# Block sums behind weight splits in the gate/up stages, and turned rows of q and y behind weight casts, in a hybrid decoder layer

## The chip, the cores and the metric

The kernel runs on one core of one Trainium2 chip. The metric is device time in microseconds (us) of one execution; the value given is the median of several. A core has five engines with a queue each: PE (TensorE, the matmuls), ACT (ScalarE), DVE (VectorE), POOL (GpSimd) and SP (SyncE, which only issues DMAs here).

## The reference

One decoder layer on 256 tokens, all in float32, model width 2048, FFN width 5632. Two half-step SwiGLU FFNs stand around a mixer of two attention branches.

```python
def _swiglu(x, w_gate, w_up, w_down):
    return (jax.nn.silu(x @ w_gate) * (x @ w_up)) @ w_down
...
    h = _layer_norm(ALPHA * h + 0.5 * _swiglu(h, ffn1_w_gate[l], ffn1_w_up[l], ffn1_w_down[l]), ln1_g[l], ln1_b[l])
    mix = _mixer(h, positions, w_in[l], ...)
    h = _layer_norm(ALPHA * h + mix, ln2_g[l], ln2_b[l])
    h = _layer_norm(ALPHA * h + 0.5 * _swiglu(h, ffn2_w_gate[l], ffn2_w_up[l], ffn2_w_down[l]), ln3_g[l], ln3_b[l])
```

The mixer projects h with w_in to queries and keys of low rank (rank 512, RMS-normed), to the queries, keys and values of a differential attention, and to two gates. Its first branch has 8 heads, each with a query of 128 plain columns and 64 rotated ones (RoPE). Its second branch has 4 heads of two score maps each, p0 - lambda * p1, with a distance bias (ALiBi). Each branch goes through an output product of its own, the two are multiplied by the sigmoid of their gates, summed to y, and y goes through w_out.

## The kernel before

**Splits.** The matmuls take operands of the type fp32r, and each float32 operand is given to them in two parts: `split` (L157) casts it on ACT to the high part (L158, CAST) and has DVE subtract that from the operand for the low part (L159, TENSOR_TENSOR). Each product is three matmuls (`triple`, L211): xh by wh (L212), xh by wl (L213), xl by wh (L214). So L213 is the first that needs the low part of a weight.

**The ring and the units.** Weights come from memory in tiles of 128 rows by 1024 columns, two blocks of 512. The split weights lie in a ring of pairs of tiles, `wring`: six pairs in the gate/up stages, ten elsewhere. A name such as `wring_16_118` is the high tile of a pair, `wring_17_119` its low tile; below, "slot 16" is the pair of the two. `next_pair` (L204) hands the pairs out in turn, so a cast into a pair has to wait until PE has done its last matmul on what the pair held. The work is cut into units. A unit has a load (a DMA on SP), a preparation (sums and split) and its matmuls; `unit` and `advance` (L177 to L203) pass it through these with a few units of lead between them, and `later(n, f)` (L107) puts a small step f behind the next n units.

**The gate/up pairs.** Each FFN has 11 pairs of a gate and an up tile of 512 columns. Pairs 1 to 10 go through the class `Hybrid` (L361). It multiplies the 2 by 2 blocks of a pair ("11", "12", "21", "22") by seven products in place of eight, as Strassen and Winograd do, and the rest of the pair by plain products. The seven products need sums of blocks, which `seventh` (L450) makes in its preparation: some by DMAs of GpSimd that accumulate (L468, L473), some on DVE (L466, in place on the loaded tile `sraw`). Six of the ten pairs (2, 3, 4, 6, 7, 8) are wide: each block has a third part, so a product with sums has three of them. The first sum belongs to the first part (s = 0), the second and the third are both issued in the preparation of the second part (s = 1). There are two such triples of sums in each wide pair.

**What sets the order.** A scheduler puts the instructions in the order of each engine's queue, by its own estimate of when they can run. `tc.issue_after(x)` adds one rule to that: what is issued inside it stands behind x if it is on the same engine. It adds no wait on another engine. `split_in_line` uses it to keep the splits on DVE in one line, and `behind_split(n)` (L354) puts an instruction behind the n-th last split. In before, each sum has `behind_split(s + 1)`. In the preparation of the second part this is the second-last split, the one ahead of the first part's. So the third sum may stand ahead of the first part's split.

**The mixer.** Rows are turned into columns by a DVE transpose of 32 by 32 blocks and a trip through memory on GpSimd's queue (`turn_out` L768, `turn` L779): a first DMA writes the blocks, a second reads them back into a tile `turned`, and a step some units later takes them. `turn_to_cols` (L792) takes them by an ACT copy (L795), for the rotated queries into `qrT` (`qr_done`, L1463) and for the keys into `kT`. `turn_to_quad` (L789) takes the rows of y by a split. The four differential heads come as steps scores, turn, values, turn2 (`diff_head`, L1402), spread over units by `later`; their exponentials are L1257 and L1258, the difference of the two maps L1420, and PE transposes the result at L1268.

Of the kernel before, what the change touches and what calls it, by code (L numbers as in the profile page):

```python
# [28 lines left out]
DH = 4  # L29
# [30 lines left out]
def layer_kernel(ctx: ExitStack, tc: tile.TileContext, a: dict, out: bass.AP):  # L60
# [6 lines left out]
    small = ctx.enter_context(tc.tile_pool(name="small", bufs=1))  # L67
# [4 lines left out]
    def nm(s):  # L72
        uid[0] += 1
        return f"{s}_{uid[0]}"

    def act_tile(shape, dt=F32, name="act"):
        return apool.tile(shape, dt, tag="act", name=nm(name), bufs=SLOTS)

    def tmp_tile(shape, name="tmp", dt=F32):
        return small.tile(shape, dt, tag="tmp", name=nm(name), bufs=6)  # L80
# [26 lines left out]
    def later(n, fn):  # L107
        uid[0] += 1
        heapq.heappush(todo, (step[0] + n, uid[0], fn))
# [45 lines left out]
    cast, lows, fetched, placed, weights = [None], [None], [None], [None], [None]  # L155
# [42 lines left out]
    def unit(load, prep, now, later_on=None):  # L198
        if load is not None:
            load()  # L200
        loaded.append((prep, now, later_on))
        advance(*ahead)

    def next_pair():  # L204
        assert len(ring) > len(prepared) + lag[0], (len(ring), len(prepared), lag[0])
        catch_up(len(ring) - 1)
        pair = ring.pop(0)
        ring.append(pair)
        return pair

    def triple(o, xh, xl, wh, wl, first, last, again=False):  # L211
        PE.matmul(o, xh, wh, start=first, stop=False, skip_group_check=again)  # L212
        PE.matmul(o, xh, wl, start=False, stop=False, skip_group_check=again)  # L213
        PE.matmul(o, xl, wh, start=False, stop=last, skip_group_check=again)  # L214
# [139 lines left out]
    def behind_split(n):  # L354
        return tc.issue_after(line[-n].ins) if len(line) >= n else nullcontext()

    def split_in_line(strict, *a):
        with behind_split(1) if strict else nullcontext():
            line.append(split(*a))

    class Hybrid:  # L361
# [42 lines left out]
        def group(self, w0, w1, done, wide=0, seeded=False, gates=False):  # L404
            banks = {}
            small = self.small
# [22 lines left out]
            def bank(n):  # L429
                first = n not in banks  # L430
                if first:
                    banks[n] = tr_bank() if n == "Z" and not small else mm_bank()
                return banks[n], first
# [9 lines left out]
            def source(name, s):  # L443
                w, j0 = blocks[name]
                return w[j0 + s] if s < 2 else w[4 + j0 // 2][:, :wide * 512]

            def stored(name, s):
                return R[name][s] if s < 2 else R[name][s][:, :wide * 512]

            def seventh(p, s):  # L450
                load_block, src, add, b = plan[p]
                st = {}
                tiles = G if s < 2 else wide

                def load():
                    if s < 2 and load_block in there:
                        return
                    nc.sync.dma_start(stored(load_block, s), source(load_block, s))

                def prep():  # L460
                    t = stored(src, s)
                    last = None
                    if add is not None:
                        for i in {0: (0,), 1: tuple(range(1, end_s + 1)), 2: ()}[s]:
                            with nullcontext() if small else behind_split(s + 1):
                                last = V.tensor_tensor(out=stored(src, i), in0=stored(src, i), in1=stored(add[1], i), op=ALU.add)  # L466
                    if p == 6 and p in added:
                        nc.gpsimd.dma_start(stored("22", s), source("12", s), accum_op=ALU.add)  # L468
                    pair = [v[:, :tiles * 512] for v in next_pair()]
                    with tc.issue_after(last.ins) if last is not None and not small else nullcontext():  # L470
                        split_in_line(not small, *pair, t)
                    if p == 1 and p in added:
                        nc.gpsimd.dma_start(stored("11", s), source("12", s), accum_op=ALU.add)  # L473
                    st["pair"] = [v.rearrange("p (g n) -> p g n", g=tiles) for v in pair]

                def now():
                    o, first = bank(b)
                    wh, wl = st["pair"]
                    for g in range(tiles):
                        if s < 2:  # L480
                            xh, xl = (v[:, 2 * s + g, :] for v in self.seven.at_[p])
                        else:
                            xh, xl = (v[:, g, :] for v in self.extra.at_[p])
                        triple(o, xh, xl, wh[:, g, :], wl[:, g, :], first and g == 0,
                               s == end_s and g == tiles - 1 and p in stops, b in "XZ" or seeded)
                    if s == end_s and p in after:
                        after[p]()
                unit(load if load_block else None, prep, now)
# [42 lines left out]
            turn = {n: iter(PLAIN[wide]) for n in range(2)}  # L531
# [236 lines left out]
    def turn_out(row, to):  # L768

        t = tmp_tile([P, 512], "blocks")  # L770
        V.transpose(t, row)  # L771
        for i in range(4):
            nc.gpsimd.dma_start(to.rearrange("(g r) (i f) -> i r g f", g=4, i=4)[i],  # L773
                                t[32 * i:32 * (i + 1), :].rearrange("r (g f) -> r g f", g=4))

    def turned(v):
        return v.rearrange("p (i k c) -> p k i c", i=4, k=4)

    def turn(row, use, wait, more):  # L779
        to = dram.tile([P, 512], F32, name=nm("turn"))  # L780
        turn_out(row, to)

        def back():
            t = tmp_tile([P, 512], "turned")
            nc.gpsimd.dma_start(t, to)
            later(more, lambda: use(turned(t)))
        later(wait, back)

    def turn_to_quad(row, b, x, q, wait, more):  # L789
        turn(row, lambda t: x.put(q, b, t), wait, more)  # L790

    def turn_to_cols(row, dst, b, wait, more, pinned=False):  # L792
        def use(t):
            with tc.issue_after(cast[0].ins) if pinned else nullcontext():
                S.copy(dst[:, :, b * P:(b + 1) * P].rearrange("p k (i c) -> p k i c", i=4), t)  # L795
        turn(row, use, wait, more)
# [432 lines left out]
    def rope(dst1, dst2, src, b, heads):  # L1229
        v = src.rearrange("p (h j i) -> p h j i", h=heads, j=2)  # L1230
        n = heads * ROPE
        tc_ = tmp_tile([P, heads, 2, HALF], "ropec")
        ts_ = tmp_tile([P, heads, 2, HALF], "ropes")
        sin = sincos[:, b, 0, :].unsqueeze(1).unsqueeze(1).to_broadcast([P, heads, 2, HALF])
        cos = sincos[:, b, 1, :].unsqueeze(1).unsqueeze(1).to_broadcast([P, heads, 2, HALF])
        V.tensor_tensor(out=tc_, in0=v, in1=cos, op=ALU.mult)
        V.tensor_tensor(out=ts_, in0=v, in1=sin, op=ALU.mult)
        V.tensor_tensor(out=dst1, in0=tc_[:, :, 0, :], in1=ts_[:, :, 1, :], op=ALU.subtract)
        V.tensor_tensor(out=dst2, in0=ts_[:, :, 0, :], in1=tc_[:, :, 1, :], op=ALU.add)
# [48 lines left out]
    def mixer(x, norm):  # L1288
# [47 lines left out]
        def cols_proj(w, xx, kt, name, k0=0, more=4, pinned=False):  # L1336
            dst = act_tile([P, 4, T], F32, name)

            def done(b, bank):
                t = tmp_tile([P, 512], name + "r")  # L1340
                S.copy(t, bank)
                later(1, lambda: turn_to_cols(t, dst, b, 4, more, pinned))
            project(w, xx, kt, 512, done, k0)
            return dst
# [111 lines left out]

        for h in range(DH):
            for i, f in enumerate(diff_head(h)):
                later(2 + 5 * h + 3 * i + i // 3, f)
        qT = [cols_proj(a["wuq"][c], cn, 4, "qT") for c in range(2)]  # L1460
        qrT = act_tile([P, 4, T], F32, "qrT")

        def qr_done(b, bank):  # L1463
            t = tmp_tile([P, 512], "qr")
            tv = t.rearrange("p (j h i) -> p j h i", j=2, h=MH)
            rope(tv[:, 0], tv[:, 1], bank, b, MH)
            later(1, lambda: turn_to_cols(t, qrT, b, 4, 4))
        project(a["wuq"][2], cn, 4, 512, qr_done)
        kT = [cols_proj(a["wuk"][c], cn, 4, "kT", 4, 6, True) for c in range(2)]
        v = [act_tile([P, 1024], F32, "v") for _ in range(2)]  # L1470
# [211 lines left out]
```

## Time and profile before

| what | us |
| --- | --- |
| median of 3 runs | 1958.54 (1957.15 to 1961.01) |
| the profiled execution | 1957.34 |
| its span | 1955.6 |
| PE busy in FFN1 up to 440 us | 438.45 of 440 |
| PE busy from 440 to 900 us | 459.69 of 460 |
| PE busy from 900 to 1340 us | 438.62 of 440 |
| PE busy from 1340 to 1700 us (FFN2's gate/up) | 359.77 of 360 |
| PE busy from 1700 us to the end | 246.45 of 255.6 |

A group row of the profile reads: line, engine, operation, written tile <- read tiles, shapes, count, then busy time and the mean of one in ns. A row of the timeline reads: start, duration, engine, line, operation, tiles, count of instructions that follow each other in the row; in brackets stands the engine's idle time before it, with what ended that. PE's matmuls overlap, so their pace is read from their starts.

### The profile page before, as it was taken

How to read it: one execution, taken by the hardware profiler on the slowest of the kernel's cores; microseconds unless marked ns; L12 is line 12 of the kernel's file. 1: busy time of each engine (PE TensorE's matmuls, PEld its weight loads, DVE VectorE, ACT ScalarE, POOL GpSimd, SP SyncE). 2: the span in 40 equal slices, each digit the busy share in tenths (PEclk: the TensorE clock that was granted, in tenths of full speed). 3: DMA queues.
4: the chain of work that ended last, by engine and by line, in shares of the span. 5: the costliest groups of instructions: out<-in, count | busy, mean ns of one | idle time of the engine just before them, and what ended most of it. 6: DMA issues, size and time to landing. Idle time of an engine off the chain costs nothing.

```text
span 1955.6 us, 25740 instructions
## 1 busy us (share of the span) xinstructions
PE 1943.0 (99%) x8715; PEld 1609.0 (82%) x8715; DVE 1760.4 (90%) x2117; ACT 1276.4 (65%) x1636; POOL 377.0 (19%) x610
## 2 busy tenths in 40 slices
PE   9999999999999999999999999999999999999998
PEld 8888888888888888888888888888888888888886
DVE  7999999999898879988987677789999999998987
ACT  6677676776655666666667655566767676666652
POOL 0122212321100010102241530012221122210110
PEclk9999999999999999999999999999999999999999
DMA  9988997988877667767676798688988888888973
GB/s 333 295 239 244 271 303 236 239 269 279 313 245 240 215 218 269 262 201 241 198 260 203 221 306 276 200 298 247 252 256 282 279 233 245 274 303 253 320 249 124
DMA packets 152244, 498.30 MB, mean 255 GB/s; under 512 B 22016, under 2 KB 22320, under 8 KB 152112
## 3 DMA queue, kind: packets, MB, share of 16 engines
q1 hardware_dynamic: 110592, 371.64, 52.9%
q0 software_dynamic: 41376, 124.89, 27.2%
q8 instruction: 68, 1.11, 0.2%
q14 instruction: 64, 0.52, 0.1%
q10 hardware_dynamic: 144, 0.13, 0.0%
HBM read 466.16 MB, written 30.41 MB: 254 GB/s over the span
## 4 chain that ended last, share of the span: by engine, by line
PE 94%; DVE 4%; DMA 1%; issue 1%; ACT 0%; SPq 0%; DVEq 0%
PE mm L213 26%; PE mm L214 26%; PE mm L212 26%; PE tr L213 4%; PE tr L214 4%; PE tr L212 4%; DVE wring L159 2%; DVE sraw L466 1%; PE tr L729 1%; DMA sraw<-in_gu_dram 0%; DMA xraw<-in_xT_dram 0%; PE tr L1483 0%; PE tr L1411 0%; PE tr L1485 0%; DMA raw<-in_gu_dram 0%
## 5 line engine op out<-in xcount | busy, mean ns | idle before, releaser
L158 ACT CAST wring<-sraw 128x1024 fp32r<-128x1024 f32 (+1 forms) x576 | 568.2, 1009 | 188.4 <-PE mm L214 69.8
L159 DVE TENSOR_TENSOR wring<-sraw,wring 128x1024 fp32r<-128x1024 f32 (+1 forms) x576 | 651.1, 1165 | 22.1 <-ACT wring L158 19.3
L158 ACT CAST wring<-raw 128x1024 fp32r<-128x1024 f32 (+2 forms) x436 | 448.7, 1035 | 281.2 <-PE mm L214 198.3
L159 DVE TENSOR_TENSOR wring<-raw,wring 128x1024 fp32r<-128x1024 f32 (+2 forms) x436 | 518.3, 1197 | 93.3 <-ACT wring L158 90.7
L212 PE MATMUL mm<-wring,h 128*128 128x512 f32 (+2 forms) x1152 | 443.5, 385 | 0.0
L213 PE MATMUL mm<-wring,h 128*128 128x512 f32 (+2 forms) x1152 | 442.7, 384 | 0.0
L214 PE MATMUL mm<-wring,h 128*128 128x512 f32 (+2 forms) x1152 | 442.6, 384 | 0.0
L212 PEld LDWEIGHTS mm<-wring,h 128*128 128x128 f32 x1152 | 216.4, 188 | 43.0 <-ACT h L158 0.8
L214 PEld LDWEIGHTS mm<-wring,h 128*128 128x128 f32 x1152 | 216.4, 188 | 42.8 <-DVE h L159 0.4
L213 PEld LDWEIGHTS mm<-wring,h 128*128 128x128 f32 x1152 | 216.4, 188 | 42.2
L213 PE MATMUL mm<-wring,xs 128*128 128x512 f32 x616 | 240.2, 390 | 0.5 <-DVE wring L159 0.5
L214 PE MATMUL mm<-wring,xs 128*128 128x512 f32 x616 | 239.7, 389 | 0.0
L212 PE MATMUL mm<-wring,xs 128*128 128x512 f32 x616 | 239.5, 389 | 0.0
L466 DVE TENSOR_TENSOR sraw<-sraw,sraw 128x1024 f32<-128x1024 f32 x168 | 191.4, 1166 | 4.1 <-DMA sraw<-in_wdk_dram 4.0
L773 POOL DMA_DIRECT2D hT<-blocks x176 | 97.5, 561 | 211.1 <-DVE blocks L771 109.4
L213 PEld LDWEIGHTS mm<-wring,xs 128*128 128x128 f32 x616 | 115.6, 188 | 26.0 <-DVE wring L159 2.1
L212 PEld LDWEIGHTS mm<-wring,xs 128*128 128x128 f32 x616 | 115.6, 188 | 24.0
L214 PEld LDWEIGHTS mm<-wring,xs 128*128 128x128 f32 x616 | 115.6, 188 | 23.9
L468 POOL DMA_DIRECT2D sraw<-in_gu_dram x60 | 52.5, 919 | 382.2 <-DVE sraw L466 355.5
L213 PE MATMUL mm<-wring,x 128*128 128x512 f32 x240 | 93.6, 391 | 0.1
L214 PE MATMUL mm<-wring,x 128*128 128x512 f32 x240 | 93.3, 390 | 0.1
L212 PE MATMUL mm<-wring,x 128*128 128x512 f32 x240 | 92.4, 390 | 0.0
(344 smaller groups left out, 2682.6 us busy)
## 6 DMA issues: line engine op xcount, KB each, us to landing
sraw<-in_gu_dram SPq DMA_DIRECT2D x156, 512.0 KB, 7.5
raw<-in_dn_dram SPq DMA_DIRECT2D x140, 512.0 KB, 4.7
raw<-in_gu_dram SPq DMA_DIRECT2D x110, 512.0 KB, 7.2
sraw<-in_gu_dram POOLq DMA_DIRECT2D x104, 512.0 KB, 7.6
sraw<-in_dn_dram SPq DMA_DIRECT2D x36, 512.0 KB, 4.8
raw<-in_w_out_dram SPq DMA_DIRECT2D x32, 512.0 KB, 4.6
hraw<-hT POOLq DMA_DIRECT2D x56, 256.0 KB, 6.2
raw<-in_wgd_dram SPq DMA_DIRECT2D x24, 512.0 KB, 4.4
```

Source lines behind the costliest of these rows:

```text
L158: cast[0] = S.copy(hi, src)
L159: lows[0] = V.tensor_tensor(out=lo, in0=src, in1=hi.bitcast(F32), op=ALU.subtract)
L212: PE.matmul(o, xh, wh, start=first, stop=False, skip_group_check=again)
L213: PE.matmul(o, xh, wl, start=False, stop=False, skip_group_check=again)
L214: PE.matmul(o, xl, wh, start=False, stop=last, skip_group_check=again)
L466: last = V.tensor_tensor(out=stored(src, i), in0=stored(src, i), in1=stored(add[1], i), op=ALU.add)
L468: nc.gpsimd.dma_start(stored("22", s), source("12", s), accum_op=ALU.add)
L729: PE.transpose(t[:, i * P:(i + 1) * P], src[:, i * P:(i + 1) * P], ident)
L773: nc.gpsimd.dma_start(to.rearrange("(g r) (i f) -> i r g f", g=4, i=4)[i], t[32 * i:32 * (i + 1), :].rearrange("r (g f) -> r g f", g=4))
```

## The change

There are four edits. First, in the wide pairs the third sum (i == 2) gets `behind_split(1)`: it stands behind the split of the first part. Second, the split of y's turned rows stands behind the last cast and the last subtraction issued. Third, the steps turn, values and turn2 of the last differential head come 2, 2 and 1 units later. Fourth, the copies of the turned q rows to qrT are taken six units after their read instead of four, and stand behind the last cast issued.

```diff
@@ -462,7 +462,7 @@
                         for i in {0: (0,), 1: tuple(range(1, end_s + 1)), 2: ()}[s]:
-                            with nullcontext() if small else behind_split(s + 1):
+                            with nullcontext() if small else behind_split(1 if i == 2 and tiles > 1 and wide > 1 else s + 1):
                                 last = V.tensor_tensor(out=stored(src, i), in0=stored(src, i), in1=stored(add[1], i), op=ALU.add)
@@ -787,7 +787,10 @@
     def turn_to_quad(row, b, x, q, wait, more):
-        turn(row, lambda t: x.put(q, b, t), wait, more)
+        def use(t):
+            with tc.issue_after(cast[0].ins), tc.issue_after(lows[0].ins):
+                x.put(q, b, t)
+        turn(row, use, wait, more)
@@ -1456,7 +1459,7 @@
             for i, f in enumerate(diff_head(h)):
-                later(2 + 5 * h + 3 * i + i // 3, f)
+                later(2 + 5 * h + 3 * i + i // 3 + (0, 2, 2, 1)[i] * (h == DH - 1), f)
@@ -1464,7 +1467,7 @@
             rope(tv[:, 0], tv[:, 1], bank, b, MH)
-            later(1, lambda: turn_to_cols(t, qrT, b, 4, 4))
+            later(1, lambda: turn_to_cols(t, qrT, b, 4, 6, True))
         project(a["wuq"][2], cn, 4, 512, qr_done)
```

Lines behind L787 are higher by 3 in the changed kernel. What each engine is given changes in order as follows.

**First place: the third pair of FFN1.** On DVE, before. The three sums write `sraw_55`, `sraw_56` and `sraw_88`, whose splits go to slots 10, 8 and 18:

```order
L466 TENSOR_TENSOR sraw_55_279<-sraw_55_279,sraw_67_339 128x1024
L466 TENSOR_TENSOR sraw_56_280<-sraw_56_280,sraw_68_340 128x1024
L466 TENSOR_TENSOR sraw_88_430<-sraw_88_430,sraw_89_431 128x1024
L159 TENSOR_TENSOR wring_11_113<-sraw_55_279,wring_10_112 128x1024
L159 TENSOR_TENSOR wring_9_111<-sraw_56_280,wring_8_110 128x1024
```

On DVE, now:

```order
L466 TENSOR_TENSOR sraw_55_279<-sraw_55_279,sraw_67_339 128x1024
L466 TENSOR_TENSOR sraw_56_280<-sraw_56_280,sraw_68_340 128x1024
L159 TENSOR_TENSOR wring_11_113<-sraw_55_279,wring_10_112 128x1024
L466 TENSOR_TENSOR sraw_88_430<-sraw_88_430,sraw_89_431 128x1024
L159 TENSOR_TENSOR wring_9_111<-sraw_56_280,wring_8_110 128x1024
```

The third sum and the first split have changed places. On ACT at the same place, before, the casts of these tiles and of the three that follow (`sraw_86`, `sraw_87`, `sraw_91`):

```order
L158 CAST wring_10_112<-sraw_55_279 128x1024
L158 CAST wring_8_110<-sraw_56_280 128x1024
L158 CAST wring_16_118<-sraw_86_428 128x1024
L158 CAST wring_18_120<-sraw_88_430 128x1024
L158 CAST wring_14_116<-sraw_87_429 128x1024
L158 CAST wring_12_114<-sraw_91_433 128x1024
```

On ACT, now:

```order
L158 CAST wring_16_118<-sraw_86_428 128x1024
L158 CAST wring_10_112<-sraw_55_279 128x1024
L158 CAST wring_8_110<-sraw_56_280 128x1024
L158 CAST wring_14_116<-sraw_87_429 128x1024
L158 CAST wring_12_114<-sraw_91_433 128x1024
L158 CAST wring_18_120<-sraw_88_430 128x1024
```

The cast of `sraw_86` into slot 16 has moved ahead of the casts of the first two sums, and the cast of the third sum has moved to the end.

**Second place: the fourth pair of FFN1.** Here the sums write `sraw_86`, `sraw_87` and `sraw_91`, and the tiles that follow are `sraw_55`, `sraw_56` and `sraw_88`. On ACT, before:

```order
L158 CAST wring_8_110<-sraw_86_428 128x1024
L158 CAST wring_14_116<-sraw_55_279 128x1024
L158 CAST wring_18_120<-sraw_87_429 128x1024
L158 CAST wring_16_118<-sraw_91_433 128x1024
L158 CAST wring_12_114<-sraw_56_280 128x1024
L158 CAST wring_10_112<-sraw_88_430 128x512
```

On ACT, now:

```order
L158 CAST wring_14_116<-sraw_55_279 128x1024
L158 CAST wring_8_110<-sraw_86_428 128x1024
L158 CAST wring_12_114<-sraw_56_280 128x1024
L158 CAST wring_18_120<-sraw_87_429 128x1024
L158 CAST wring_10_112<-sraw_88_430 128x512
L158 CAST wring_16_118<-sraw_91_433 128x1024
```

The casts of the following tiles now alternate with those of the sums, each one place ahead. DVE's order there changes as at the first place.

**Third place: the third differential head.** On ACT, before, with `qrT` taken from `turned_1042`; the exponentials write p, `kT` is the next turned copy:

```order
L158 CAST wring_549_5032<-raw_1155_8436 128x1024
L795 COPY qrT_947_7822<-turned_1042_8099 128x4x128
L1257 ACT_TABLE_LOAD
L1257 ACTIVATE p_1058_8149,sums_1059_8150<-st_1055_8142,nmx_1057_8147 128x128
L1258 ACTIVATE p_1058_8149,sums_1059_8150<-st_1055_8142,nmx_1057_8147 128x256
L158 CAST wring_16_118<-raw_1156_8453 128x1024
L795 COPY kT_968_7888<-turned_1069_8178 128x4x128
```

On ACT, now:

```order
L158 CAST wring_549_5032<-raw_1153_8430 128x1024
L1260 ACT_TABLE_LOAD
L1260 ACTIVATE p_1058_8149,sums_1059_8150<-st_1055_8142,nmx_1057_8147 128x128
L1261 ACTIVATE p_1058_8149,sums_1059_8150<-st_1055_8142,nmx_1057_8147 128x256
L158 CAST wring_16_118<-raw_1154_8447 128x1024
L798 COPY kT_968_7888<-turned_1069_8178 128x4x128
```

The copy of `turned_1042` is no longer ahead of the exponentials; it stands 16 rows further down, behind two casts of `od`.

## The prediction

> **What bounds the kernel now.** I read the page first: the span, the busy times and the chain that ended last.
>
> ```profile
> span 1955.6 us, 25740 instructions
> PE 1943.0 (99%) x8715; PEld 1609.0 (82%) x8715; DVE 1760.4 (90%) x2117; ACT 1276.4 (65%) x1636; POOL 377.0 (19%) x610
> PE 94%; DVE 4%; DMA 1%; issue 1%; ACT 0%; SPq 0%; DVEq 0%
> ```
>
> PE (TensorE) is busy for 99% of the span and is 94% of the chain. The change takes no matmul away, so it can win only what PE waits. The list of PE's waits says how much that is:
>
> ```profile
> PE tr L931 <- ACT pair L929: 4.1, 1, 4.1
> PE tr L1268 <- DVE p L1420: 1.1, 1, 1.1
> ...
> PE mm L213 <- DVE wring L159: 0.5, 2, 0.3
> ```
>
> The 4.1 us lie at the end of the kernel, which the change doesn't touch. The 1.1 us lie in the mixer, and 0.5 us are two waits for a weight split. So the most that can be won is small. What can be lost is not bounded so. The table by stretches, for the gate/up stage of FFN1 and of FFN2, has the columns us, PE, PEld, DVE, ACT, POOL busy, clock, DMA share and GB/s:
>
> ```profile
> 62.00:440.00 378.00, 377.73 (x1666) 312.06 (x1665) 372.25 (x394) 272.83 (x327) 97.52 (x144) 1.00 0.88 260
> 1340.00:1700.00 360.00, 359.77 (x1586) 297.17 (x1585) 354.36 (x374) 256.82 (x308) 86.55 (x129) 1.00 0.88 263
> ```
>
> In FFN1's 378 us DVE is idle for 5.75 us, in FFN2's 360 us for 5.64 us. It is nearly as full as PE, so a wait of DVE there is soon a wait of PE. The list of ACT's (ScalarE's) waits gives the other half:
>
> ```profile
> ACT wring L158 <- PE mm L214: 268.1, 292, 5.8
> ```
>
> ACT has time, but its casts wait 268.1 us in all for PE to release a ring slot. What stands behind such a cast in ACT's order starts only after it (part 2 has a copy of this kind that waits 1.50 us, and the exponential behind it with it).
>
> **Part 1: the third sum.** The edit asks that the third block sum (L466) stand behind the split of the first. No instruction is added; in the order it moves at six places in each FFN (the other six triples of sums in each stood so already). At a place DVE's order goes from sum, sum, sum, split to sum, sum, split, sum. But the split needs its cast first, and there ACT's order changes too. Take the third pair of FFN1, near 143 us (the first place in the order section): ACT, DVE, then PE.
>
> ```profile
> 141.16 5.98 ACT L158 CAST wring<-sraw 128x1024 fp32r<-128x1024 f32 x6 [1.85 <-DVE sraw L466]
> 139.91 3.49 DVE L466 TENSOR_TENSOR sraw<-sraw,sraw 128x1024 f32<-128x1024 f32 x3
> 143.31 6.90 DVE L159 TENSOR_TENSOR wring<-sraw,wring 128x1024 fp32r<-128x1024 f32 x6
> 142.37 0.39 PE L214 MATMUL tr<-wring,xs 128*128 128x512 f32 x1
> 145.54 0.39 PE L213 MATMUL mm<-wring,xs 128*128 128x512 f32 x1
> 146.90 0.39 PE L213 MATMUL mm<-wring,xs 128*128 128x512 f32 x1
> 148.26 0.39 PE L213 MATMUL mm<-wring,xe 128*128 128x512 f32 x1
> ```
>
> ```profile
> L159 DVE TENSOR_TENSOR wring<-sraw,wring 128x1024 fp32r<-128x1024 f32 x520 | 617.7, 1216 | 21.1 <-ACT wring L158 18.3
> ```
>
> Prices: a cast 5.98 / 6 = 1.0 us; a sum 3.49 / 3 = 1.16; a split 1.2, or 1.15 (6.90 / 6) in a run of them. The six starts from 145.54 to 146.90 make PE's pace 0.227 us. In before, DVE is never idle here: sums to 143.31, then the splits of 55, 56 and 88. The first ends at about 144.5, and PE wants its low half at 145.54; the third one's low half is wanted at 148.26, so 1.0 to 1.5 us are in hand.
>
> In after, ACT's queue has the cast of 86 into slot 16 ahead of the cast of 55. PE's last matmul on slot 16 is the one at 142.37, so the slot is free at 142.76. Cast 86 then runs to 143.8, cast 55 to 144.8, 56 to 145.8, 87 and 91 to 147.7, 88 to 148.7. DVE has done two sums by 142.25 and stands until 144.85: the third sum, which would have filled the time, is now behind split 55. Split 55 ends at 146.05, the third sum at 147.2, split 56 at 148.4, and split 88, after its cast, at 149.9. PE's new order puts one matmul more ahead of the first two needs and two ahead of the third, 0.23 us each: PE is late by 146.05 - 145.77 = 0.3, then 148.4 - 147.13 = 1.3, then 149.9 - 148.7 = 1.2. These aren't added, the largest counts: **+1.3 us**.
>
> The fourth pair, near 184 us, runs the same way (the second place in the order section): DVE, then PE.
>
> ```profile
> 180.68 3.48 DVE L466 TENSOR_TENSOR sraw<-sraw,sraw 128x1024 f32<-128x1024 f32 x3
> 184.09 6.36 DVE L159 TENSOR_TENSOR wring<-sraw,wring 128x1024 fp32r<-128x1024 f32 x6
> 181.81 0.39 PE L214 MATMUL tr<-wring,xs 128*128 128x512 f32 x1
> 184.76 0.61 PE L212 MATMUL mm<-wring,xs 128*128 128x512 f32 x2
> 185.35 0.50 PE L213 MATMUL mm<-wring,xs 128*128 128x512 f32 x1
> 186.85 0.39 PE L213 MATMUL mm<-wring,xs 128*128 128x512 f32 x1
> ```
>
> Now the cast of 55 into slot 14 stands ahead of the cast of 86. PE leaves slot 14 at 182.20, so cast 55 runs to 183.2 and 86 to 184.2. Split 86 runs 184.25 to 185.45, where it began at 184.09 before: the sum taken from in front of it gains nothing, the split is even later. The third sum ends at 186.6 and split 87, wanted at 186.85, at 187.8: **+0.95 us**. In before this place already cost PE a little: the matmul at 185.35 starts 0.59 after the pair of L212, where two starts take 0.45.
>
> The last wide pair, near 343 us, has the same exchange on ACT: ACT, then PE.
>
> ```profile
> 340.26 5.55 ACT L158 CAST wring<-sraw 128x1024 fp32r<-128x1024 f32 x6 [2.24 <-DVE sraw L466]
> 341.09 0.39 PE L214 MATMUL tr<-wring,xs 128*128 128x512 f32 x1
> 344.26 0.39 PE L213 MATMUL mm<-wring,xs 128*128 128x512 f32 x1
> 345.62 0.39 PE L213 MATMUL mm<-wring,xs 128*128 128x512 f32 x1
> ```
>
> Slot 14 is free at 341.48; cast 55 ends at 342.5, cast 86 at 343.5. Split 86 ends at 344.75, the third sum at 345.9, split 87 at 347.1. It is wanted at 345.62 + 0.23: **+1.25 us**.
>
> The other three places of this FFN (near 160, 205 and 364 us) have smaller exchanges. At 205 a wait goes, which the profile shows; FFN2 has its like:
>
> ```profile
> 205.64 0.50 PE L213 MATMUL mm<-wring,xs 128*128 128x512 f32 x1 [0.27 <-DVE wring L159]
> 1470.33 0.50 PE L213 MATMUL mm<-wring,xs 128*128 128x512 f32 x1 [0.23 <-DVE wring L159]
> ```
>
> By the same walk I take +0.15, -0.25 and +0.4, together +0.3 us; bounds are -0.8 (these places lose every small wait) and +1.2 (each is late by a third of a split). So FFN1 comes to 1.3 + 0.95 + 1.25 + 0.3 = 3.8 us. FFN2 has the same exchanges in its order and nearly the same idle time of DVE, so **7.6 us** for both. Bounds: from below -1.5, all four short stalls of this kind gone (an estimate, a quarter to half a us each, about what the rows show idle and the slower matmul behind it); from above 14, where each of the 12 places is late by one sum (1.16). I take 7.6, as the slots' release is read off PE, which is at pace. The DMA accumulates follow the sums; the third landing of a place comes at most one split and its wait later, and I take 0.
>
> **Part 2: the turned rows of q.** qrT's copy moves behind a weight cast and two units later, on ACT in front of the exponentials of the third diff head (the third place in the order section). ACT, GpSimd, the DMA row, and PE:
>
> ```profile
> 1031.14 0.62 ACT L795 COPY qrT<-turned 128x512 f32<-128x512 f32 x1 [1.50 <-DMA turned<-turn]
> 1034.88 0.62 ACT L795 COPY kT<-turned 128x512 f32<-128x512 f32 x1
> 1035.41 0.40 ACT L1257 ACTIVATE p<-st,nmx 128x128 f32<-128x128 f32 x1
> 1028.54 0.56 POOL L785 DMA_DIRECT2D turned<-turn  x1
> turned<-turn POOLq DMA_DIRECT2D x26, 256.0 KB, 4.2
> 1036.32 0.39 PE L214 MATMUL mm<-wring,h 128*128 128x512 f32 x1
> 1037.85 0.30 PE L1268 MATMUL tr<-ident,p 128*128 128x128 f32 x1 [1.15 <-DVE p L1420]
> ```
>
> The copy waits 1.50 us for its DMA, and the exponentials behind it with it; PE then waits at L1268, starting at 1037.85 where its pace says 1036.55: 1.3 us. With the copy gone ACT is 1.5 + 0.6 us earlier. Next late is the kT copy, whose rows were asked for at 1028.54 and land 4.2 us later, about 1032.8 or a little after; with the copy and what else stands there the exponential behind it starts near 1034.1 instead of 1035.41, and the chain reaches L1268 about 1.3 us earlier: **-1.3 us**. Bounds: -1.3 and 0 (kT's rows land as late as the copy runs now).
>
> **Part 3: the rest.** The last diff head's steps come one or two units later; their transposes and two copies stand behind weight casts that PE needs anyway, and the output product that reads them starts many units after. y's turned rows get an edge, and no row moves on any engine. Both 0; if the head were late, at most one wait like that at L1268, +1.1.
>
> **Sum.** 1957.34 (the profiled execution; 1.7 us around its span) + 7.6 - 1.3 = 1963.6. The median of before, 1958.54, is 1.2 above that execution, so **1964.8 us**, 0.32% slower. A measurement here can tell about 0.2% (3.9 us) from no change.
>
> **Rivals.**
> *The edit does what it says* (the other side: not slower). Split and sum change places and ACT's casts lie in slots free in time: the four short stalls (1.5) and the mixer's 1.3 go: 1957.34 - 2.8 + 1.2 = 1955.7, no change that can be told. For it: DVE is what PE waits for in those rows. Against: the casts' new order and the slots' times. It decides where the moved casts find their slot free before the sums end (142.25 at the first place, against 142.76).
> *Cover.* PE, late by 1.3 us after the first place, gives DVE that time for the next ones; only one debt per FFN stays: 2 x 1.3 - 1.3 = +1.3, so 1957.34 + 1.3 + 1.2 = 1959.8. Against: ACT's 268.1 us of waits for PE tie casts to PE, so a late PE makes a late slot.
> *The change does nothing at the sums*, as PE is at pace over them: 1958.54 - 1.3 = 1957.2. Against: 1.0 to 1.5 us in hand, less than the 2.6 us that DVE stands.
> *The clock falls.* The waits of PE become frequent, and the granted clock with them. The rows of the stretch after the 1.1 us wait and of that after the 4.1 us wait:
>
> ```profile
> 1038.00:1042.00 4.00, 4.00 (x20) 3.30 (x20) 3.36 (x10) 3.75 (x6) 0.00 (x0) 1.00 0.80 298
> 1948.80:1950.00 1.20, 0.78 (x2) 0.49 (x3) 1.17 (x2) 0.28 (x2) 0.00 (x0) 0.50 0.34 128
> ```
>
> After 1.1 us the clock is whole, after 4.1 us it is half. If each of the six long new waits brought the half clock for as long as 4 us, it would cost 2 us each: +12, so 1977. The Trainium skill (TensorE: Matmul & The Clock Gate, HAM oscillation — how this bites in real kernels) says that PE idle for over some 3.4 us falls back to the half clock, and that waits which recur can do so each time. By that rule this change keeps the clock, as none of its waits is over 1.5 us; the two rows agree.
>
> **Chances.** Forecast 0.62; the edit does what it says 0.15; cover 0.12; nothing 0.06; clock 0.05. Range: the forecast's bounds reach from 1957 (half its debts) to 1970 (FFN places at 1.0 each); with the first rival it is 1955.5 to 1970.0, which leaves out under 0.15. Faster than 1954.6: 0.04. Within: 0.15 + 0.12 + 0.06 less that, and the forecast's lower end (under 1962.4) with 0.05: 0.34. Slower: 0.62.
>
> **What would show it.** In after's profile near 143 us DVE stands 2.6 us ahead of split 55, with ACT's cast as the releaser, ACT's first cast starts at 142.8, and PE L213 waits for DVE's split at the three long places of each FFN, 0.3 to 1.3 us each. PE's waits for DVE wring rise from 0.5 to about 8 us, and L1268's 1.1 us go. It is wrong if those waits don't rise, if the casts find free slots, or if a DMA is what PE waits for.

## The result and the profile after

The changed kernel takes 1966.05 us (median of 6 runs, 1965.52 to 1967.29) where before takes 1958.44 (6 runs, 1957.15 to 1961.01). The ratio is 1.004, with a 95% interval of 1.0029 to 1.005: 7.6 us slower. Its profiled execution has these first lines on the page, and these of PE's waits:

```profile
span 1964.1 us, 25760 instructions
PE 1946.8 (99%) x8715; PEld 1608.4 (82%) x8715; DVE 1762.0 (90%) x2117; ACT 1277.0 (65%) x1638; POOL 377.0 (19%) x610
PE 94%; DVE 2%; ACT 1%; DMA 1%; issue 1%; POOL 0%; SPq 0%; DVEq 0%; ACTq 0%
```

```profile
PE mm L213 <- DVE wring L159: 5.5, 16, 0.6
PE tr L934 <- ACT pair L932: 4.1, 1, 4.1
...
PE tr L1502 <- DMA pt<-pturn: 0.7, 1, 0.7
```

The engines did the same work: 8715 matmuls, the same counts on DVE, and two table loads more on ACT. PE waits 16 times for a weight's low half where it waited twice. The wait for p at the third differential head (L1268, now L1271) has left the list, and a wait for pt has come.

The first place near 143 us, on ACT, DVE and PE:

```profile
142.47 5.79 ACT L158 CAST wring<-sraw 128x1024 fp32r<-128x1024 f32 x6 [3.01 <-PE tr L214]
```

```profile
141.32 2.35 DVE L466 TENSOR_TENSOR sraw<-sraw,sraw 128x1024 f32<-128x1024 f32 x2
144.50 1.23 DVE L159 TENSOR_TENSOR wring<-sraw,wring 128x1024 fp32r<-128x1024 f32 x1 [0.83 <-ACT wring L158]
145.65 1.22 DVE L466 TENSOR_TENSOR sraw<-sraw,sraw 128x1024 f32<-128x1024 f32 x1
146.78 1.22 DVE L159 TENSOR_TENSOR wring<-sraw,wring 128x1024 fp32r<-128x1024 f32 x1
```

```profile
145.78 0.50 PE L213 MATMUL mm<-wring,xs 128*128 128x512 f32 x1 [0.18 <-DVE wring L159]
...
147.05 0.40 PE L212 MATMUL mm<-wring,xs 128*128 128x512 f32 x1
148.06 0.50 PE L213 MATMUL mm<-wring,xs 128*128 128x512 f32 x1 [0.61 <-DVE wring L159]
148.39 0.40 PE L214 MATMUL mm<-wring,xs 128*128 128x512 f32 x1
```

The bracket of the cast is what to read first. In before the first cast waited for a sum of DVE; now it waits 3.01 us for PE, which still reads slot 16. DVE then waits 0.83 us for the cast of `sraw_55`, which stands behind, and the third sum lies between the two splits that PE needs. PE waits for both.

The price is more than the brackets say. From 147.05 to 148.06 there are 1.01 us where the pace is 0.23, and the matmul after takes 0.33 to follow: 0.9 us lost for a listed wait of 0.61. So I read the loss from the matmuls' starts: the start of the n-th matmul less that of the n-th in before (a running median over 13, since a few matmuls change places). It grows by what a stretch loses:

| stretch | after less before, us |
| --- | --- |
| 140 to 152 us (first place) | +1.41 |
| 152 to 176 | +0.30 |
| 176 to 203 (second place) | +1.10 |
| 203 to 335 | -0.08 |
| 335 to 355 (last wide pair) | +1.41 |
| 355 to 372 | +0.47 |
| 372 to 1025 | 0.0 |
| 1025 to 1045 (third differential head) | -1.19 |
| 1045 to 1340 (rest of the mixer) | +1.22 |
| 1340 to 1700 (FFN2's gate/up) | +4.57 |

FFN1's places lose 4.61 us and FFN2's 4.57. Before the first place the kernel is 0.33 us ahead, which is the start of the execution, and varies (from 0.4 ahead to 0.7 behind in the kernels below).

**Places that lose nothing.** The starts of the sums on DVE show that the third sum moved behind the first split at eight places of each FFN, and not at six. At three of the eight, near 103, 265 and 305 us in FFN1, nothing is lost. DVE's order changed there in the same way, but ACT's first cast still waits for a sum of DVE and not for PE:

```profile
101.02 3.14 ACT L158 CAST wring<-sraw 128x1024 fp32r<-128x1024 f32 x3 [1.48 <-DVE sraw L466]
262.74 2.19 ACT L158 CAST wring<-sraw 128x1024 fp32r<-128x1024 f32 x2 [1.19 <-DVE sraw L466]
302.84 6.00 ACT L158 CAST wring<-sraw 128x1024 fp32r<-128x1024 f32 x6 [1.85 <-DVE sraw L466]
```

Near 165 us it is the other way round. The sums and splits on DVE stand as in before, but on ACT the first sum's cast now comes behind the cast of a `raw` tile that waits 2.34 us for PE, and 0.30 us are lost. So already in this one trace the loss goes with the order on ACT and not with the exchange on DVE.

### The profile page after: what moved, and what is told of

Its sections match the earlier page's. It is cut to its first block, busy times and chain, and to the rows that moved or that the text cites. A ratio compares the mean times of both kernels' runs of the same rounds, so it can differ in the third digit from the quotient of the medians.

```text
span 1964.1 us, 25760 instructions
## 1 busy us (share of the span) xinstructions
PE 1946.8 (99%) x8715; PEld 1608.4 (82%) x8715; DVE 1762.0 (90%) x2117; ACT 1277.0 (65%) x1638; POOL 377.0 (19%) x610
## 4 chain that ended last, share of the span: by engine, by line
PE 94%; DVE 2%; ACT 1%; DMA 1%; issue 1%; POOL 0%; SPq 0%; DVEq 0%; ACTq 0%
PE mm L213 27%; PE mm L214 27%; PE mm L212 26%; PE tr L214 4%; PE tr L213 4%; PE tr L212 4%; ACT wring L158 1%; DVE wring L159 1%; PE tr L729 1%; DMA pt<-pturn 0%; DMA xraw<-in_xT_dram 0%; DVE sraw L466 0%; DMA gate<-gates 0%; PE tr L1414 0%; PE tr L1486 0%
## 5 line engine op out<-in xcount | busy, mean ns | idle before, releaser
L158 ACT CAST wring<-sraw 128x1024 fp32r<-128x1024 f32 (+1 forms) x576 | 566.4, 1009 | 193.9 <-PE mm L214 86.1
L158 ACT CAST wring<-raw 128x1024 fp32r<-128x1024 f32 (+2 forms) x436 | 448.4, 1034 | 286.9 <-PE mm L214 203.7
L213 PE MATMUL mm<-wring,h 128*128 128x512 f32 (+2 forms) x1152 | 442.8, 385 | 0.0
L213 PEld LDWEIGHTS mm<-wring,h 128*128 128x128 f32 x1152 | 216.4, 188 | 42.1
L213 PE MATMUL mm<-wring,xs 128*128 128x512 f32 x616 | 241.8, 392 | 5.5 <-DVE wring L159 5.5
L213 PEld LDWEIGHTS mm<-wring,xs 128*128 128x128 f32 x616 | 115.6, 188 | 36.7 <-DVE wring L159 13.0
L213 PE MATMUL mm<-wring,x 128*128 128x512 f32 x240 | 93.3, 390 | 0.1
```

The lines of the kernel that those rows point to most:

```text
L158: cast[0] = S.copy(hi, src)
```

## The experiments

Each kernel was run with a profile, and most were timed in five rounds with before. Before's median was 1957.55, 1958.04 and 1958.23 us in the three sets of rounds, so a kernel is compared by its ratio to before in its own set. "In the gate/up stages", "at the third head" and so on are stretches of the table's kind, read from the profiled execution.

### One edit at a time

The third sum's edit alone is the first hunk of the diff, and the rest as before:

> The third sum's edit alone, the other three edits undone. Theory (the edit costs by the order of the casts on ACT, at six places of each FFN): all of the gate/up loss is here, 4.6 us in FFN1 and 4.5 in FFN2 by the changed kernel's trace, so 9 us over before, 1967.5, with the same late splits near 143, 185, 344 us and their like in FFN2. Rival (the mixer's edits bring half of the loss): 4 to 5 us over before.

Measured: 1968.17 us, ratio 1.0053 (1.0041 to 1.0066). The gate/up stages lose 4.55 and 4.64 us, at the same places and by the same steps. The cast at the first place is released by the same thing:

```profile
143.47 5.79 ACT L158 CAST wring<-sraw 128x1024 fp32r<-128x1024 f32 x6 [3.01 <-PE tr L214]
```

So this edit alone makes the loss in the gate/up stages. By the interval it costs 8 to 13 us, which holds the expected 9 and not the rival's 4 to 5. In this profile 0.73 us are lost at the third head as well.

The other three edits without it:

> All edits but the third sum's. Theory (the wait of PE for pt near 1137 us in the changed kernel comes from the shift of the last differential head's steps): -1.2 us at the third differential head, +0.9 at the wait for pt, +0.3 between 1049 and 1073 us, so 0 us against before, 1958.5. Rival (that wait is chance, or comes from the FFN's delay): -1.0 us, 1957.5, and no wait for pt.

Measured: 1957.22 us, ratio 0.9999 (0.999 to 1.0008). At the third head -0.90, between there and 1340 us +0.28, in the gate/up stages 0. The wait for pt isn't there. The interval (2 us below before to 1.6 above) holds the theory's time and the rival's, so the time doesn't decide. The terms do: the theory's +0.9 is missing, and what came is nearer the rival's.

The three edits one by one. The turned q rows (the fourth hunk of the diff):

> The edit of the turned q rows alone: on ACT one copy moves, nothing else. Theory: the wait of PE for the third differential head's p near 1037 us goes, -1.2 us, 1957.3, and PE's wait for pt does not come. Rival (it only makes room for the wait for pt behind it): 0 us, with a wait of PE for pt of about 0.7 us near 1130 us.

Measured: 1956.79 us, ratio 0.9992 (0.9984 to 1.0001). At the third head -1.25 us, and no wait for pt. (Beside the copy on ACT, some of PE's small products between 1052 and 1060 us changed places too.) The last head's shift (the third hunk), in two runs of the same kernel:

> The shift of the last differential head's steps alone. It moves DMAs on GpSimd's queue: reads of pt now stand ahead of writes of the gates. Theory: this brings the wait of PE for pt near 1130 us, +0.9 us, and the drift of 0.3 us between 1049 and 1073 us, so +1.2 us, 1959.7. Rival (the wait for pt is chance or needs the FFN's delay): 0 us and no wait for pt.

> The shift of the last differential head's steps alone, a second profile. The first one has PE waits of 0.8 us for a gate product near 1180 us and 1.6 us for the third head's p near 1037. Theory (both are landings that differ between executions): the wait near 1180 is not there again and that near 1037 comes out otherwise by 0.3 us or more. Rival (the shift makes them): the same two waits within 0.2 us.

Measured: 1958.75 us, ratio 1.0004 (0.9995 to 1.0013), and 1956.31 in the one timing of the second. PE's waits in the two profiles, the first run and then the second:

```profile
PE tr L1268 <- DVE p L1420: 1.6, 1, 1.6
...
PE tr L729 <- DVE diff L1537: 0.8, 1, 0.8
```

```profile
PE tr L1268 <- DVE p L1420: 0.2, 1, 0.2
```

The wait for a gate product (L1537) is in the one and not in the other, and the wait for p is 1.6 and 0.2 us long, in one and the same kernel. Behind both are landings: the cast of y's turned rows (L158), ahead of the gate product, waits 3.53 us for its DMA in the first run and 0.74 in the second, and the copy to qrT, ahead of the exponentials, 1.97 and 0.22. Neither run has a wait for pt, so the larger term of the first theory didn't come. What came both times is the drift between 1049 and 1073 us, +0.22 us. The edit of y's rows (the second hunk) moves no instruction:

> The edit of the turned rows of y alone. No instruction moves on any engine against before, so every theory expects 0 us; what it shows beside that is how far two timings of the same order lie apart.

Measured: 1957.67 us, ratio 0.9996 (0.9987 to 1.0005). Its matmuls keep time with before's from 62 us to the end but for 0.4 us, as expected.

### The order of the casts

Here the casts are put in line too: each weight cast of `split_in_line` stands behind the one before it on ACT, in the order of the units. Once with the third sum's edit, once without:

```diff
     def split_in_line(strict, *a):
-        with behind_split(1) if strict else nullcontext():
+        with behind_split(1) if strict else nullcontext(), tc.issue_after(casts[-1].ins) if strict and casts else nullcontext():
             line.append(split(*a))
+        casts.append(cast[0])
```

> The third sum's edit alone, and beside it each weight cast of the gate/up stage stands behind the cast before it, in the order of the units. DVE keeps the changed order sum, sum, split, sum; ACT's casts come 55, 56, 88, 86, 87, 91 at the first place. Theory (the casts' order makes the loss): no split is late, the four short waits of before go, -1.5 us, 1957.0. Rival (the exchange on DVE itself makes the loss, since a sum now stands ahead of the second split): the splits of the second and third tile are late as in the changed kernel, 5 us or more over before, 1963 or more.

> Before, with each weight cast of the gate/up stage behind the cast before it; the sums as in before. Both theories: 0 us against before, within 0.5, since a cast that leaves its place ahead of the third sum's cast was not the one that a split waited for. It serves to tell the casts' line from the exchange on DVE: a difference to the kernel with both is the exchange's alone, -1.5 us by the theory.

With the third sum's edit: 1956.37 us, ratio 0.9997 (0.9988 to 1.0006). The first place, on ACT and on DVE:

```profile
141.37 2.18 ACT L158 CAST wring<-sraw 128x1024 fp32r<-128x1024 f32 x2 [1.93 <-DVE sraw L468]
144.90 3.91 ACT L158 CAST wring<-sraw 128x1024 fp32r<-128x1024 f32 x4 [1.35 <-DVE sraw L468]
```

```profile
140.12 2.35 DVE L468 TENSOR_TENSOR sraw<-sraw,sraw 128x1024 f32<-128x1024 f32 x2
142.45 1.23 DVE L159 TENSOR_TENSOR wring<-sraw,wring 128x1024 fp32r<-128x1024 f32 x1
143.59 1.22 DVE L468 TENSOR_TENSOR sraw<-sraw,sraw 128x1024 f32<-128x1024 f32 x1
144.73 5.89 DVE L159 TENSOR_TENSOR wring<-sraw,wring 128x1024 fp32r<-128x1024 f32 x5
```

DVE's order is sum, sum, split, sum, as in the changed kernel, and DVE has no wait. The casts are released by sums again. The loss of 4.6 us in each FFN is a gain of 0.84. That settles the rival: the exchange on DVE doesn't make the loss, the casts' order does. (The time itself can't be told from before's: the interval holds 1. The gain is read from the matmuls' starts, here and for the next kernel.)

Without the third sum's edit the line gives 1956.65 us, ratio 0.9993 (0.9984 to 1.0002), and the same -0.84 and -0.83 us in the gate/up stages. I had expected 0. So the four short waits of before were not cured by the exchange either: the line cures them, and the exchange is worth nothing beside it. In FFN1 the line wins 0.28 us near 185 us and 0.56 near 205, the two places of these waits. DVE near 165 us, in before and then with the line alone, shows how:

```profile
167.65 1.23 DVE L159 TENSOR_TENSOR wring<-sraw,wring 128x1024 fp32r<-128x1024 f32 x1 [1.15 <-ACT wring L158]
...
180.68 3.48 DVE L466 TENSOR_TENSOR sraw<-sraw,sraw 128x1024 f32<-128x1024 f32 x3
```

```profile
164.91 2.49 DVE L159 TENSOR_TENSOR wring<-sraw,wring 128x1024 fp32r<-128x1024 f32 x2
167.31 1.22 DVE L159 TENSOR_TENSOR wring<-raw,wring 128x1024 fp32r<-128x1024 f32 x1
...
179.19 3.49 DVE L468 TENSOR_TENSOR sraw<-sraw,sraw 128x1024 f32<-128x1024 f32 x3
```

Already in before, a pair earlier, DVE waits 1.15 us for a cast. With the line it doesn't, and the three sums begin at 179.19 and not at 180.68. That is 1.5 us sooner, or 1.1 without the 0.4 us by which this execution is ahead from its start, and the split behind them is in time.

### The versions that might be best

The line of casts with the turned q rows, with the sums' edit and without:

> The third sum's edit with the casts in line, and the edit of the turned q rows; neither the head's shift nor the edit of y. Theory: -1.5 us in the gate/up stages and -1.2 at the third differential head, so 1955.7, the shortest of all kernels here. Rival (the exchange on DVE makes the loss): 4 us or more over before, 1962 or more.

> Casts of the gate/up stage in line and the edit of the turned q rows; the sums as in before. The earlier run of the line without the sums' edit lost the four short waits by itself, so theory now (the exchange on DVE is worth nothing): -1.4 us in the gate/up stages and -0.9 to -1.3 at the third head, like the kernel with the sums' edit as well, 1955.0, within 0.5. Rival (the exchange is worth a gain of its own): 1 us or more slower than that kernel.

Measured: 1955.04 us, ratio 0.9985 (0.9976 to 0.9993), with it; 1956.12 us, ratio 0.9988 (0.9979 to 0.9997), without. Both are faster than before beyond their intervals, by 2 to 3 us. The second missed its expected 1955.0 within 0.5, and its median is 1.1 us above the first one's, as the rival said. But they were timed in different sets, and their ratios, 0.0003 apart, can't be told apart. In the gate/up stages, where the exchange is, both gain 0.83 to 0.85 us in each FFN, so its term isn't there. The second one's profile loses 2.2 us between 940 and 1010 us, with a wait of 0.8 us near 944 that no other kernel shows. At the third head they gain 0.86 and 1.10 us; but the line alone, without the edit of the q rows, gained 1.09 there, so the runs don't show what that edit adds to the line.

### The wait for pt

> The changed kernel as it is, a second profile. The first one has a wait of PE for pt (L1502 at 1137 us, 0.7 us) that neither the kernel without the third sum's edit nor the third sum's edit alone has. Theory (it is a landing on GpSimd's queue that comes late in one execution): it is not at this place again, while the late splits of the gate/up stages come again, 4.6 and 4.5 us, within 0.2. Rival (it belongs to the four edits together): 0.5 to 1 us at L1502 again.

> The changed kernel without the shift of the last differential head. Theory: the gate/up stages lose 9 us, the third differential head gains about 1.2, so 1966; it can't be told from the changed kernel, and PE waits for no pt. Rival (the shift costs 1 us or more): 1 us below the changed kernel.

The second profile of the changed kernel (1966.5 us) has no wait for pt; the places in its gate/up stages lose 4.55 and 4.56 us again, and 0.5 us more go near 440 us, where the first profile loses nothing. The kernel without the head's shift takes 1966.2 us, ratio 1.0048 (1.0036 to 1.0061), no faster than the changed kernel. The list of PE's waits in its profile, whose execution was the longest of the five (1970.33 us):

```profile
PE tr L729 <- DVE diff L1540: 1.6, 1, 1.6
...
PE tr L1502 <- DMA pt<-pturn: 0.7, 1, 0.7
```

It has the wait for pt without the shift. I had expected it to be absent here, and that failed. So the wait comes in one execution of the changed kernel and not in another, and it doesn't need the shift. It is in two of the three profiles that have the edits of the sums, y and q together without the line of casts, and in none of the other eleven. Whether these edits make it likelier, and what delays the landing, stays open.

## Why the prediction was right, step by step

**The bound.** PE is the bound before and after, and little was there to be won. That held.

**The casts at the slots.** This step carried the forecast, and the trace shows it nearly to the tenth. Put on before's time by the delay that had gathered by then, the first cast starts at 142.80 at the first place (142.47 + 0.33; said 142.8), at 182.23 at the second and at 341.52 at the last wide pair (the slots were said to be free at 182.20 and 341.48), each where PE leaves the slot. The rows of the last two, in after:

```profile
183.61 5.48 ACT L158 CAST wring<-sraw 128x1024 fp32r<-128x1024 f32 x6 [2.67 <-PE tr L214]
```

```profile
343.92 5.48 ACT L158 CAST wring<-sraw 128x1024 fp32r<-128x1024 f32 x6 [3.01 <-PE tr L214]
```

**DVE's wait.** I had DVE stand 2.6 us at the first place; it stands 0.83. Its sums begin at 141.32 where before they began at 139.91: from 133 us on, one split and one row of `gus` (L1005) more stand ahead of them. The split's time doesn't hang on that: split 55 began at 144.83 on before's time, where 144.85 was said, since its cast sets it.

**The size per place.** Said and measured: first place +1.3 and +1.41; second +0.95 and +1.10; last wide pair +1.25 and +1.41; near 160 us +0.15 and +0.30; near 205 -0.25 and -0.08; near 364 +0.4 and +0.47. In all 3.8 and 4.6 us in FFN1, and the same in FFN2, as the like order had said. All six are short by 0.1 to 0.2 us. I had PE go on the instant that a split ended and at its pace; in the rows it starts some 0.05 us later, and the next matmul follows after 0.33 us and not 0.23. That is this term's mis-sizing: +7.6 said, +9.2 measured. For the same reason PE's listed waits for DVE's splits came to 5.5 us and not to about 8: the list holds only part of what a late split costs.

**The number of places.** The third sum moves at eight places of each FFN and not at six, and near 160 us it stands as in before. The prediction priced the six at which time changes, and the three that it left out cost nothing, so its sum didn't suffer; but a reader who counts on the exchange alone would have priced the wrong places. The lower end of its range doesn't follow from its reason either: half of the debts is 3.8 us, and 1957.34 + 3.8 - 1.3 + 1.2 is 1961.0, not 1957. The forecast itself doesn't hang on that.

**The third head.** -1.3 said, -1.19 here. The next thing late was the kT copy, as said; it waits for its landing now:

```profile
1037.98 0.62 ACT L798 COPY kT<-turned 128x512 f32<-128x512 f32 x1 [0.80 <-DMA turned<-turn]
```

But the price came from one execution. In the profiles without this edit PE's wait for p is 1.1 us (before), 1.9 (the third sum alone), 1.2 (y's rows alone), 1.6 and 0.2 (the head's shift), 0.5 and none (the line with and without the sums' edit). With the edit it is none, 0.2, 0.2, none, none, 0.3 and 0.5. The means are 0.9 and 0.2 us: the edit is worth about 0.8 us of wait, an estimate from these, or 1.1 without the kernels that have the line of casts. The single values lie so far apart that -1.3 is neither confirmed nor refuted as a mean. That -1.19 came so near it is in part luck: the second run of the head's shift and the line alone, which don't have the edit, gain 0.94 and 1.09 us there too, with a copy to qrT that waits 0.22 and 0.40 us for its landing where before's waited 1.50.

**The rest at 0.** The shift of the last head is not 0 but +0.2 us: between 1049 and 1073 us the profiles that have it lose 0.22 to 0.26, those with the q rows' edit alone of the two about 0.1, and the others nothing. The prediction overlooked that the shift moves DMAs on GpSimd's queue. By the traces, reads of pt now stand ahead of three writes of pturn between 1078 and 1094 us; the writes of the gates, which the expectation of that run names, keep their place there. The wait for pt, +0.95 in the first profile, doesn't need the shift; its cause is open.

**The sum.** +9.2 - 1.2 + 1.2 in the rest of the mixer, less the 0.3 of the start, make 8.9 us up to the 4.1 us wait at the end. The last two matmuls behind that wait bring 0.4 back, since the granted clock there is 1.00 in after and 0.50 in before, and the spans lie 8.5 us apart. The medians lie 7.6 apart, since before's profiled execution was 1.1 us below its median and the changed kernel's 0.1. So the time said, 1964.8, was 1.2 short: the gate/up term was too small by 1.6, and the rest is what differs between executions.

**The rivals.** That the edit does what it says needed casts that find their slot free; they don't. And the kernel with casts in line shows that this rival would not have had its gain from the exchange. Cover did not happen: each place loses as much in FFN2 as in FFN1, and those behind an earlier loss lose no less than was said of each by itself. The clock stayed at 1.00 through the new waits, as the forecast had it. The row that was to show what a long wait does, the one behind the 4.1 us, doesn't repeat: in after the clock behind the same wait is whole. Over the 1.2 us behind it the granted clock is 0.50 to 0.62 in twelve of the fourteen profiles, and 1.00 in after and in the q rows alone. The rows at the first place and behind the long wait, in after:

```profile
142.00:152.00 10.00, 9.21 (x39) 6.96 (x39) 8.88 (x9) 8.69 (x10) 3.44 (x4) 1.00 0.77 136
...
1957.70:1958.90 1.20, 0.78 (x3) 0.41 (x3) 1.17 (x2) 0.28 (x2) 0.00 (x0) 1.00 0.34 126
```

## What to carry to other kernels

An edge that orders one engine's queue can reorder another's: compare the order of every engine on the two sides of a dependence, and look for an instruction that now heads its queue while what it writes into is still being read. Such a head can be priced before any run: the time at which the last reader ends, from the trace of before, and everything behind it from there. Where PE then waits, add what it needs to get back to its pace (0.1 to 0.2 us a place here). A wait that is a landing must be read from more than one profile before its removal is priced.

## What the runs showed beside that

A listed wait of PE of 0.61 us cost 0.9 us by the matmuls' starts, and in all 5.5 us listed stand beside 9.2 us lost. Two profiles of one kernel agree within 0.1 us over the places of both gate/up stages, and differ in the mixer by 0.7 to 1.4 us in single waits that hang on landings of GpSimd's queue. The kernel without the head's shift also has a wait of 0.84 us near 510 us that no other has (PE's L213 for a split on DVE); its cause is open.
